# A channel shuffle on one core: two early tiles stored in pieces, large tiles moved as even and odd partitions

## The chip, the core and the metric

The kernel runs on one core of a Trainium2 chip. The metric is the device time of one execution in microseconds (us); lower is better. KB in this text is 1024 bytes and, where a tile or a piece is named by its size, it is the size per partition: a "38 KB tile" has 38 KB in each of the 128 partitions, 4864 KB in all.

## The reference

```python
def reference(x, groups):                 # x: (16, 64, 64, 256) float32, groups = 8
    batch, h, w, c = x.shape
    channels_per_group = c // groups      # 32
    x = x.reshape(batch, h, w, groups, channels_per_group)
    x = x.transpose(0, 1, 2, 4, 3)
    return x.reshape(batch, h, w, c)
```

Each of the 65,536 pixels has 256 channels (1 KB). They are taken as an 8 by 32 matrix and transposed to 32 by 8. Nothing is added or multiplied: 67.11 MB are read from HBM, permuted inside every 1 KB row, and 67.11 MB are written back.

## The kernel before, in words

The pixels lie one after another in HBM and are cut into slots, `_SLOTS = [[4, 8], [28]] + [[38]] * 12 + [[16]]`. A slot's number is how many pixels each of the 128 partitions holds, so that a 38 slot is one tile of 38 KB in each partition, and partition p's 38 KB are contiguous in HBM. The numbers add up to 512 pixels per partition, which is the whole input. The first slot has two parts of 4 and 8 KB in one tile.

For every slot there is an `in_tile` from a pool of two buffers (`_IN_BUFS`) and an `out_tile` from a pool of three (`_OUT_BUFS`). Each part goes through three steps:

- L55, issued by SyncE (SP): one DMA loads the part from HBM into `in_tile`.
- L57, VectorE (DVE): one copy from `in_tile` to `out_tile` does the permutation, by its access patterns.
- L61, issued by ScalarE (ACT): one DMA stores the part from `out_tile` to HBM.

Nothing is put in order by hand beyond that (`tc.manual_schedule(engines=None)`): every engine takes its own instructions in the order in which the loop issues them, and the framework adds the waits. It finds them from the parts of tiles that instructions read and write. A load into a buffer waits for the copy that read it two slots earlier. A copy waits for its load, and for the store that read its `out_tile` buffer three slots earlier. A store waits for its copy. A DMA reports that it has landed on one of eight semaphores (`DMAHW0` to `DMAHW7`), which are used again and again; a DMA that takes one over waits until the DMA that had it last has landed.

SP and ACT have a DMA queue each (q1 carries the loads, q10 the stores), and both queues are served by the same 16 DMA engines. A DMA of 128 partitions is cut into 128 packets, one for each partition, 8 on each engine, and ends with a 4-byte packet on each engine that counts the semaphore up.

Of the kernel before, what the change touches and what calls it, by code (L numbers as in the profile page):

```python
# [1 line left out]

# [4 lines left out]


F32 = mybir.dt.float32
P = 128  # L10

_SLOTS = [[4, 8], [28]] + [[38]] * 12 + [[16]]
_IN_BUFS = 2
_OUT_BUFS = 3


@with_exitstack
def kernel(
    ctx: ExitStack,
    tc: tile.TileContext,  # L20
    x: bass.AP,
    groups: bass.AP,
    out: bass.AP,
):
    nc = tc.nc
    b, h, w, c = x.shape
    G = int(groups)
    CPG = c // G
    assert G * CPG == c
    assert sum(map(sum, _SLOTS)) * P == b * h * w  # L30
    biggest = max(map(sum, _SLOTS))

    x_flat = x.rearrange("b h w c -> (b h w c)")
    out_flat = out.rearrange("b h w c -> (b h w c)")

    in_pool = ctx.enter_context(tc.tile_pool(name="in_pool", bufs=_IN_BUFS))
    out_pool = ctx.enter_context(tc.tile_pool(name="out_pool", bufs=_OUT_BUFS))

    def rows(flat, first, q):

        return flat[first * c : (first + P * q) * c].rearrange("(p f) -> p f", p=P)

    ctx.enter_context(tc.manual_schedule(engines=None))
    first = 0
    for parts in _SLOTS:
        in_tile = in_pool.tile([P, biggest * c], F32, name="in_tile")
        out_tile = out_pool.tile([P, biggest * c], F32, name="out_tile")
        at = 0
        pieces = []
        for q in parts:  # L50
            pieces.append((q, first, slice(at * c, (at + q) * c)))
            first += P * q
            at += q
        for q, start, cols in pieces:
            nc.sync.dma_start(out=in_tile[:, cols], in_=rows(x_flat, start, q))  # L55
        for q, start, cols in pieces:
            nc.vector.tensor_copy(  # L57
                out=out_tile[:, cols].rearrange("p (i j g) -> p i j g", j=CPG, g=G),
                in_=in_tile[:, cols].rearrange("p (i g j) -> p i j g", g=G, j=CPG),
            )  # L60
            nc.scalar.dma_start(  # L61
                out=rows(out_flat, start, q), in_=out_tile[:, cols]
            )


# [1 line left out]
_INS = ['x', 'groups']  # L67
_OUTS = [((16, 64, 64, 256), 'float32')]

_NUMBERS = {'groups': 8}  # L70


# [26 lines left out]
```

## Time and profile before

| what | value |
|---|---|
| median of 3 runs | 316.21 us (316.19 to 316.47) |
| span of the profiled execution, first to last instruction | 314.4 us |
| last DMA packet ends, last completion arrives (from the span's start) | 313.3 us, 313.6 us |
| VectorE busy | 119.0 us, 38%, 16 copies |
| DMA engines busy, loads and stores | 49.8% and 49.4% of the span |
| moved | 134.22 MB, mean 427 GB/s |

The span is the profiled execution's own time between its first and last instruction. The page has no second clock around it; the median of the runs lies 1.8 us above the span, and that difference is taken as what lies around the span in every execution. VectorE is idle most of the time, and all of that idle time ends with a load that lands. Times below are counted from the span's start.

### The profile page before, as it was taken

Reading aid. Unit: us, or ns where it says so; the run is one execution under the profiler, and the core shown is the slowest. Engines: PE = TensorE matmul, PEld = TensorE weight load, DVE = VectorE, ACT = ScalarE, POOL = GpSimd, SP = SyncE. Lnnn points to the kernel's source line nnn. Section 1 sums busy time; section 2 is a strip of 40 time slices with the busy share of each in tenths; the row PEclk is TensorE's granted clock in tenths of the full one; section 3 lists DMA queues with packets and bytes.
Section 4 is the critical chain, followed back from the end, with each engine's and each line's share of the span. In section 5 each row is a group of like instructions: output and inputs, shape, how many; then the busy total and the mean of one; then the engine's idle time right before and its main releaser. Section 6 shows DMA issues by size and latency. Waiting matters only on the chain.

```text
span 314.4 us, 132 instructions
## 1 busy us (share of the span) xinstructions
DVE 119.0 (38%) x16; POOL 0.2 (0%) x4
## 2 busy tenths in 40 slices
DVE  2081907309109109019028028037046055065400
POOL 0000000000000000000000000000000000000000
DMA  7999999999999999999999999999999999999997
GB/s 317 405 441 416 435 416 483 401 465 406 450 421 446 426 436 436 401 470 396 475 396 475 396 470 401 470 401 470 401 450 421 446 426 436 436 417 450 429 421 321
DMA packets 4608, 134.22 MB, mean 427 GB/s; under 512 B 512, under 2 KB 512, under 8 KB 768
## 3 DMA queue, kind: packets, MB, share of 16 engines
q1 hardware_dynamic: 2304, 67.11, 49.8%
q10 hardware_dynamic: 2304, 67.11, 49.4%
HBM read 67.11 MB, written 67.11 MB: 427 GB/s over the span
## 4 chain that ended last, share of the span: by engine, by line
DMA 76%; DVE 19%; issue 0%; SPq 0%; DVEq 0%
DMA in_tile<-in_x_dram 76%; DVE out_tile L57 19%; SPq L55 0%; DVEq L57 0%
## 5 line engine op out<-in xcount | busy, mean ns | idle before, releaser
L57 DVE COPY out_tile<-in_tile 128x9728 f32<-128x9728 f32 (+4 forms) x16 | 119.0, 7440 | 179.4 <-DMA in_tile<-in_x_dram 179.4
L80 POOL MEMSET const-uint8-127<- 128x1 uint8 x1 | 0.1, 103 | 0.0
L80 POOL MEMSET const-bfloat16-1.0<- 128x1 bf16 x1 | 0.1, 102 | 0.0
L80 POOL MEMSET const-float32-1.0<- 128x1 f32 x1 | 0.1, 100 | 0.0
L80 POOL MEMSET const-float32-0.0<- 128x1 f32 x1 | 0.1, 99 | 0.2 <-issue 0.2
## 6 DMA issues: line engine op xcount, KB each, us to landing
in_tile<-in_x_dram SPq DMA_DIRECT2D x12, 4864.0 KB, 37.0
out_dram<-out_tile ACTq DMA_DIRECT2D x12, 4864.0 KB, 42.6
in_tile<-in_x_dram SPq DMA_DIRECT2D x1, 3584.0 KB, 14.7
out_dram<-out_tile ACTq DMA_DIRECT2D x1, 3584.0 KB, 30.9
in_tile<-in_x_dram SPq DMA_DIRECT2D x1, 2048.0 KB, 30.4
out_dram<-out_tile ACTq DMA_DIRECT2D x1, 2048.0 KB, 15.2
in_tile<-in_x_dram SPq DMA_DIRECT2D x1, 1024.0 KB, 5.4
out_dram<-out_tile ACTq DMA_DIRECT2D x1, 1024.0 KB, 25.0
```

The costliest lines, as they stand in the source:

```text
L57: nc.vector.tensor_copy(out=out_tile[:, cols].rearrange("p (i j g) -> p i j g", j=CPG, g=G), in_=in_tile[:, cols].rearrange("p (i g j) -> ...
L80: nc = _bacc.Bacc("TRN2", target_bir_lowering=False, num_devices=1)
```

## The change

Two things change, on the way into and out of SBUF.

A dictionary `_CUTS = {2: [12, 16], 3: [16, 22]}` names the third part (the 28 KB tile) and the fourth (the first 38 KB tile). Each of them is still loaded as a whole, and is then copied and stored in two pieces: copy of 12 KB, its store, copy of 16 KB, its store; and 16 and 22 KB for the first 38 KB tile.

Every 38 KB tile is loaded by two DMAs, one for the 64 even partitions and one for the 64 odd ones, and is stored by two, the odd ones first. The copies still cover all 128 partitions. Loads have 28 DMAs where they had 16, stores 31 where they had 16, and there are 18 copies where there were 16.

```diff
+_CUTS = {2: [12, 16], 3: [16, 22]}
...
+    def classes(q):
+
+        if q < biggest:
+            return [slice(0, P)]
+        return [slice(0, P, 2), slice(1, P, 2)]
...
+    done = []
     for parts in _SLOTS:
...
         for q, start, cols in pieces:
-            nc.sync.dma_start(out=in_tile[:, cols], in_=rows(x_flat, start, q))
+            source = rows(x_flat, start, q)
+            for rank in classes(q):
+                nc.sync.dma_start(out=in_tile[rank, cols], in_=source[rank, :])
         for q, start, cols in pieces:
-            nc.vector.tensor_copy(
-                out=out_tile[:, cols].rearrange("p (i j g) -> p i j g", j=CPG, g=G),
-                in_=in_tile[:, cols].rearrange("p (i g j) -> p i j g", g=G, j=CPG),
-            )
-            nc.scalar.dma_start(
-                out=rows(out_flat, start, q), in_=out_tile[:, cols]
-            )
+            target = rows(out_flat, start, q)
+            lo = 0
+            for width in _CUTS.get(len(done), [q]):
+                part = slice(cols.start + lo * c, cols.start + (lo + width) * c)
+                nc.vector.tensor_copy(
+                    out=out_tile[:, part].rearrange(
+                        "p (i j g) -> p i j g", j=CPG, g=G
+                    ),
+                    in_=in_tile[:, part].rearrange(
+                        "p (i g j) -> p i j g", g=G, j=CPG
+                    ),
+                )
+                for rank in reversed(classes(q)):
+                    nc.scalar.dma_start(
+                        out=target[rank, lo * c : (lo + width) * c],
+                        in_=out_tile[rank, part],
+                    )
+                lo += width
+            assert lo == q
+            done.append(q)
```

In the changed kernel the loads are at L65, the copies at L71 and the stores at L80.

## The prediction

> **What bounds the kernel now.** I read the page first, then the chain of work that ended last, the copies by shape, and the packet records of the trace. On the page the two queue rows matter most.
>
> ```profile
> span 314.4 us, 132 instructions
> ...
> DVE 119.0 (38%) x16; POOL 0.2 (0%) x4
> ...
> DMA  7999999999999999999999999999999999999997
> GB/s 317 405 441 416 435 416 483 401 465 406 450 421 446 426 436 436 401 470 396 475 396 475 396 470 401 470 401 470 401 450 421 446 426 436 436 417 450 429 421 321
> ...
> q1 hardware_dynamic: 2304, 67.11, 49.8%
> q10 hardware_dynamic: 2304, 67.11, 49.4%
> ```
>
> The packets take 49.8% + 49.4% = 99.2% of 16 engines' span, 311.9 us of 314.4. The DMA engines never starve except in the first and the last of the 40 slices. What is idle, 2.5 us, is mostly the way to the first packet (1.75 us in the packet records) and the end. The engines are the bound; VectorE is busy 38% and costs nothing as long as the queues hold work. Same bytes, same packets: the loads cost 0.4 points (1.26 us) more than the stores. The packet records place this in the first 21 us, where loads run with few stores beside them; after that a 38 KB packet takes 1.44 us either way.
>
> From the stores' row an engine set that is never idle moves 67.11 MB in 0.494 x 314.4 = 155.3 us, 432 GB/s: 1 KB in each of 128 partitions is 0.303 us, a 38 KB tile 11.5 us.
>
> The chain shows what the queues hold when a copy runs:
>
> ```profile
> 8.66 21.50 DMA in_tile<-in_x_dram
> 30.16 0.02 issue
> 30.18 8.83 DVE out_tile L57
> 39.02 0.02 issue
> 39.03 32.20 DMA in_tile<-in_x_dram
> ```
>
> The first 38 KB tile is copied from 30.18 to 39.0, and only then is the third 38 KB load issued. That costs nothing, because the second 38 KB load is in flight (its copy starts at 49.11 in the timeline) and the stores of the 8 and 28 KB parts are queued. This cover is what I ask after for the changed kernel.
>
> ```profile
> L57 DVE COPY out_tile<-in_tile 128x9728 f32<-128x9728 f32 x12 | 105.5, 8791 | 158.5 <-DMA in_tile<-in_x_dram 158.5
> L57 DVE COPY out_tile<-in_tile 128x7168 f32<-128x7168 f32 x1 | 6.6, 6569 | 7.7 <-DMA in_tile<-in_x_dram 7.7
> L57 DVE COPY out_tile<-in_tile 128x4096 f32<-128x4096 f32 x1 | 3.9, 3873 | 7.6 <-DMA in_tile<-in_x_dram 7.6
> ```
>
> These rows (busy us, mean ns of one) price the pieces: 16 KB (4096 elements) 3.87 us; 22 KB (5632) between the rows of 4096 and 7168, 3.87 + 1536 x 0.878 ns = 5.22 us.
>
> **The change, part by part.** *More DMAs and packets.* 59 DMAs instead of 32: 27 more, each with one 4-byte completion packet per engine, 9 ns in the packet records: 0.24 us. The cut tiles have 16 more data packets per engine: two packets of 12 and 16 KB (459 ns by line between 309 and 611, and 611) against one of 28 KB (1062) cost 8 ns more, 16 + 22 against 38 KB about 10 ns: 8 x 18 ns = 0.14 us. Sum 0.38 us, all of it on the bound. Below nothing is excluded, since packets are only added.
>
> *More issues.* One DMA instruction takes 0.33 us on SP and 0.36 us on ACT (the rows of L55 and L61): 12 more on SP, 15 more on ACT. Behind an extra load on SP stands the next load, which waits for a copy anyway, and four packets of 1.44 us per engine of the first half are queued by then; behind an extra store, the next store, some 20 us away. Nothing, and without this cover 0.33 to 0.36 us each.
>
> [...] 32 DMAs back to back leave 0.8% of the span idle, so a completion is not paid at the queue while another DMA is queued. [...]
>
> *The pieces of the 28 KB tile.* Copy of 12 KB, then 16 KB without a wait; the stores go behind that of 8 KB. Order changes, not bytes: 0.
>
> *The pieces of the first 38 KB tile.* Here the instructions of the built program have something that the diff does not show. Rows 3 to 7 of VectorE and 5 and 6 of ACT, with what each waits for:
>
> ```
> 3 L71 TensorCopy out_tile<-in_tile 128x3072 [waits DMAHW3_49]
> 4 L71 TensorCopy out_tile<-in_tile 128x4096
> 5 L71 TensorCopy out_tile<-in_tile 128x4096 [waits DMAHW5_49,DMAHW0_49]
> 6 L71 TensorCopy out_tile<-in_tile 128x5632 [waits DMAHW3_49,DMAHW2_49]
> ...
> 5 L80 DMACopy out_dram<-out_tile 64x4096 [waits DMAHW2_49,DVE_49]
> 6 L80 DMACopy out_dram<-out_tile 64x4096 [waits DMAHW3_49]
> ```
>
> The 22 KB copy (row 6) waits for DMAHW3 and DMAHW2 at 32, their second completion: the even and the odd half of the 16 KB piece's store. It writes other columns than the store reads, so the data don't ask for it; the 28 KB tile's second copy, beside a store of whole partitions, has no such wait. So the 22 KB copy starts when the 16 KB store has *landed*. Behind it on VectorE stands every later copy, and so the second tile's store; SP's third 38 KB load waits for this copy (it frees the in_tile buffer), ACT's next store is its own. All that can still move before it: loads of 4, 8, 28, 38, 38 KB and stores of 4, 8, 12, 16, 16 KB. That is 172 KB x 0.303 = 52.1 us. With the first packet at 1.75 and the 1.26 us that early loads cost, the engines run dry at 55.1. VectorE is long ready: the 16 KB copy ends at 30.2 + 3.9 = 34.1, and its store is last in the queue. The second load's odd half takes over the semaphore of the 8 KB store, which landed at 8.66 + 25.0 = 33.6 before; four packets of its even half are queued beyond that: 0.
>
> Then nothing moves: last packet to completion 0.34 (313.28 to 313.62 in the packet records at the end), semaphores on VectorE 0.09 (0.04 + 0.05 in the chain's rows), the copy 5.22, 0.02, and from the next issue to its first packet 1.02 (issue at 0.73, packet at 1.75). Sum 6.69 us with all 16 engines idle. By the bounds of landing (0.02 as in the chain's "issue" rows; 0.9 if engines end as far apart as the last 1.1 us of the span allow) 6.4 to 7.3. No cover gives it back: the engines are the bound to the end. After it, load 3 (11.5 us) and the 22 KB store (6.7) make 18.2 us of work, while the copy of load 2, 8.8 us, ends and issues more.
>
> *Waits in the steady part.* A store now takes over the semaphore of the store two tiles back. Tiles come every 23.0 us (copies at 94.33 and 117.35), stores land 42.6 us after issue, so 46 - 42.6 = 3.4 us remain; if they are used up, the previous store is still queued: 0.
>
> *Half the partitions.* No row shows a DMA of 64 partitions. A 38 KB packet stays a contiguous 38 KB row, and 64 rows make four per engine if all 16 take part. Nearest row: 1.439 us for 1536 store packets, almost without spread. I take that: 0. A gain is excluded, as packets already run at the engine's constant time; for a loss the next rows are the slowed early loads, 1.09 against 1.06 us, 3%.
>
> Sum against the profiled execution: 314.4 + 0.38 + 6.69 = 321.5 us of span; with 1.8 us around it, against the median, 316.21 + 7.07 = 323.3 us.
>
> **The rivals.** *Halves run slower* (0.12). The halves carry 12 tiles x 2 x 11.5 = 276 us of engine time, so 1% is 2.8 us and 3% 8.3 us: 326 to 332, more if engines get in each other's way. For it: nothing measured speaks on 64 partitions. Against it: packets keep size and number. [...]
>
> *The pieces pay* (0.03, the other side). If stores that start earlier mix in while loads run alone, the 1.26 us vanish: 316.21 - 1.26 + 0.38 = 315.3. It decides only if the 22 KB copy's wait is free, that is if 6.7 us of other work were queued at 55 us; what I count there is none. *The wait is satisfied early and nothing else moves* (0.03): 316.6, within 0.2%. For these speaks that the wait stands in no line of the diff; against both, the built rows.
>
> **How the numbers follow.** The drained queue has 0.82; its own range is 322.6 to 324.2. The predicted time is its 323.3. The range adds 0.8 below for a store order that leaves work over, and reaches into the slower halves up to 328; beyond it I leave 0.06 below and some 0.07 above. About 0.2% (0.6 us) is what a measurement can tell from no change: faster 0.03, same 0.03, slower 0.94.
>
> **What would show it.** Right: the DMA row, all nines now, has a hole of 6 to 7 us between about 55 and 62 us, in slices 6 and 7; a 22 KB copy of 5.2 us whose wait, put down to DMA out_dram<-out_tile, is some 21 us; the queue shares sum to about 312.3 us; 38 KB packets stay at 1.44 us. Wrong: no hole (the wait is free), a second hole later (a semaphore taken over late), or queue shares above 313 us (halves run slower).

## The result and the profile after

The changed kernel takes 327.31 us (median of 4 runs, 327.15 to 327.43) against 316.20 us: slower, ratio 1.0348, 95% interval 1.0334 to 1.0363. It is 11.1 us longer. (In this text medians are over all runs of a kernel, and ratios with their intervals over its fast runs alone, those within 1.5% of its fastest.) The prediction, 323.3 us, had the direction and the place, and 7.1 of the 11.1 us.

The page of the changed kernel, the lines that answer to those of before:

```profile
span 325.5 us, 176 instructions
...
DVE 120.1 (37%) x18; POOL 0.2 (0%) x4
...
DMA  8989997399999999999999999999999999999995
GB/s 334 443 370 456 427 417 324 115 416 405 461 411 435 411 445 435 407 450 445 402 454 435 407 459 435 407 459 435 407 459 435 407 454 435 411 457 404 464 408 256
...
q1 hardware_dynamic: 2496, 67.11, 48.8%
q10 hardware_dynamic: 2800, 67.11, 47.8%
```

A slice is 8.1 us, and slices are counted from 0. The DMA row, before all nines but for its two ends, falls to 7 and 3 in slices 6 and 7, from 48.8 to 65.1 us, and ends with a 5 where it ended with a 7. The queues' packets took 96.6% of 325.5 us, 314.4 us, where they took 311.9.

The chain of waits of the changed kernel between 34 and 63 us (start, length, what) shows the hole from inside:

```profile
34.52 0.52 ACTq L80
35.04 0.04 issue
35.08 20.85 DMA out_dram<-out_tile
...
56.02 5.26 DVE out_tile L71
61.29 0.02 issue
61.30 0.47 SPq L65
61.78 0.04 issue
61.82 20.33 DMA in_tile<-in_x_dram
```

The 16 KB piece's store (two DMAs, one for each half) is issued from 34.52 on and has landed at 55.93; only then does the 22 KB copy run; only after that copy is the next load issued. The list of waits names it too: VectorE waited for a store once, for 21.5 us.

```profile
DVE out_tile L71 <- DMA in_tile<-in_x_dram: 167.6, 15, 15.0
DVE out_tile L71 <- DMA out_dram<-out_tile: 21.5, 1, 21.5
```

The stretches around it (length, busy time of VectorE and GpSimd, clock, DMA share, GB/s):

```profile
48.00:56.00 8.00, 0.00 (x0) 0.00 (x0) 1.00 0.88 377
56.00:64.00 8.00, 7.98 (x2) 0.00 (x0) 1.00 0.29 78
64.00:72.00 8.00, 5.93 (x1) 0.00 (x0) 1.00 0.91 369
```

From 56 to 64 us VectorE is busy all the time and the DMA engines for 29% of it: for this once the engines wait for VectorE, for the 5.25 us of its 22 KB copy.

I split the 11.1 us by the packet records of the two profiles, as time of all 16 engines (sums over packets divided by 16). The records name no engine: what is said of single engines here and below is read from the order in which packets start and from the last 16 completion packets.

| term | before | after | more |
|---|---|---|---|
| engines idle near 55 us | 0 | 7.4 us | 7.4 |
| load packets beyond the usual time of their size (38 KB: 1.439 us) | 1.1 | 3.2 | 2.0 |
| engines idle at the end, behind the last one | 0.3 | 1.6 | 1.3 |
| more packets and completions | | | 0.4 |

The second and third terms were not in the prediction. Of the 2.0 us, 1.3 lie between 60 and 80 us: the first 16 load packets after the hole take 1.7 to 2.8 us each instead of 1.44. At the end twelve engines are done by 322.4 us and four at 323.3 to 324.2; before, all 16 ended between 312.85 and 313.28.

### The profile page after: what moved, and what is told of

Same layout as the page of the kernel before. It is cut to its first block, busy times and chain, and to the rows that moved or that the text cites. A ratio compares the mean times of both kernels' runs of the same rounds, so it can differ in the third digit from the quotient of the medians.

```text
span 325.5 us, 176 instructions
## 1 busy us (share of the span) xinstructions
DVE 120.1 (37%) x18; POOL 0.2 (0%) x4
## 3 DMA queue, kind: packets, MB, share of 16 engines
q1 hardware_dynamic: 2496, 67.11, 48.8%
## 4 chain that ended last, share of the span: by engine, by line
DMA 75%; DVE 18%; SPq 1%; issue 0%; ACTq 0%; DVEq 0%
DMA in_tile<-in_x_dram 69%; DVE out_tile L71 18%; DMA out_dram<-out_tile 6%; SPq L65 1%; ACTq L80 0%; DVEq L71 0%
## 5 line engine op out<-in xcount | busy, mean ns | idle before, releaser
L71 DVE COPY out_tile<-in_tile 128x9728 f32<-128x9728 f32 (+5 forms) x18 | 120.1, 6682 | 189.2 <-DMA in_tile<-in_x_dram 167.6
```

Source lines behind the costliest of these rows:

```text
L71: nc.vector.tensor_copy(out=out_tile[:, part].rearrange("p (i j g) -> p i j g", j=CPG, g=G), in_=in_tile[:, part].rearrange("p (i g j) -> ...
```

## The experiments

Two theories on what lies beside the hole. Theory A: it belongs to the restart, and more widely to any stretch in which the load queue runs dry and all engines take up loads again. Theory B: it belongs to the half-partition DMAs. Each kernel was timed beside the kernel before on the same chip.

**The halves alone.** `_CUTS = {}`.

> The changed kernel without the two cuts: every 38 KB tile still moves as even and odd partitions, swapped for stores. In the changed kernel the copy's wait left the DMA engines idle for 7.4 us; 4 us more are lost elsewhere: 38 KB load packets after that hole take up to 2.8 us instead of 1.44 (2.0 us of 16 engines in sum) and the last engine ends 1.3 us later behind the others than before. Theory A (restart): both come from the restart after the hole, when all 16 engines begin loads together. Then halves alone cost only their 24 extra completions, 0.22 us: 316.4 us, no hole, 38 KB loads at a mean of 1.445 us as before. Theory B (halves): engines that carry half the partitions get in each other's way whenever loads run in step. Then 317.5 to 319.5 us, no hole, 38 KB load packets over 1.5 us in some number, engines ending over 1 us apart.

Measured: 316.17 us, ratio 0.9997 (0.9988 to 1.0005). The queue rows of its page:

```profile
span 314.4 us, 168 instructions
...
DMA  8999999999999999999999999999999999999997
...
q1 hardware_dynamic: 2496, 67.11, 49.8%
q10 hardware_dynamic: 2496, 67.11, 49.5%
```

24 more DMAs raise the stores' share by 0.1 point and nothing else. The 38 KB loads have a mean of 1.443 us, and all engines end within 0.5 us. Theory B falls for even and odd halves as this change moves them.

**The pieces alone.** `classes()` returns the whole 128 partitions always; both cuts stay.

> Only the cuts: the 28 KB and the first 38 KB tile copied and stored in pieces, every DMA over all 128 partitions. No copy of a second piece waits for the first piece's store in the built program. Both theories: no hole; 16 more data packets per engine (0.14 us) and 2 more DMAs (0.02 us) against at most 1.2 us of slowed early loads that earlier stores could relieve: 316.3, between 315.4 and 316.5 us.

Measured: 318.25 us (single runs 317.1 to 321.9), ratio 1.0065 (1.004 to 1.009). A miss for both theories as I had put them: no hole, no halves, and still 2.1 us. The list of waits of this kernel:

```profile
DVE out_tile L69 <- DMA in_tile<-in_x_dram: 130.5, 12, 16.6
DVE out_tile L69 <- DMA out_dram<-out_tile: 37.1, 3, 22.9
```

Copies wait for stores here, up to 22.9 us: an `out_tile` is not free. The reason lies in turns. Where both queues hold work, the records show an engine taking a load packet, a store packet, a load packet, whatever their sizes, with now and then two of a kind in a row: in the kernel before, five times from 34.6 to 47.1 us, 16 store packets of 28 KB start and then 16 load packets of 38 KB; in the changed kernel, from 32.96 to 36.9 us, 16 of 12 KB and then 16 of 38 KB, twice. Whole, the 28 KB tile's store has 8 packets per engine; in two pieces it has 16, and each lets a 38 KB load pass. Its chain of waits:

```profile
23.08 42.34 DMA out_dram<-out_tile
65.43 0.03 issue
65.45 0.05 DVEq L69
65.50 0.04 issue
65.55 8.84 DVE out_tile L69
```

The 16 KB rest of the 28 KB tile, issued at 23.1, lands at 65.4; the whole tile before landed 30.9 us after its issue at 22.9, at 53.8. The second 38 KB cut adds to it, and the copy that needs the `out_tile` of the first 38 KB tile starts at 97.26. The loads meanwhile have run ahead into both `in_tile` buffers: in the records no 38 KB load packet is active from 95.0 to 110.9 us. The stores go on: the copies at 97.26 and 108.68 us had both waited for one to land. But after it load packets beyond 1.5 us appear again (0.5 us in sum), some stores too (0.3 us), and one engine ends 1.2 us behind the other fifteen.

**The change without the false wait.** The stores of the first 38 KB tile's pieces go over 128 partitions.

```diff
-                for rank in reversed(classes(q)):
+                for rank in reversed(classes(width)):
```

> The whole change except that the two pieces of the first 38 KB tile are stored over all 128 partitions, so that the 22 KB copy no longer waits for the 16 KB store; everything else moves as even and odd partitions. My account of the hole: the 7.4 us go, and nothing else is late in their place. Theory A (restart): the rest goes with it, 316.6 us. Theory B (halves): some of the 4 us stay, 317.5 to 320 us. If the hole had another cause, it stays near 327.

Measured: 318.05 us, ratio 1.0055 (1.0043 to 1.0067). The hole is gone and 9.3 of the 11.1 us with it, which shows that the wait was its cause. The loads run dry twice here, from 53 to 61 and from 80 to 85 us, while the stores go on, and two engines end 1.6 to 1.8 us behind the rest. What holds these loads back is a store too: SyncE waited for one three times, up to 21.9 us, before it issued a load. The first 16 load packets after the two stretches took 1.44 to 1.46 us, not the 1.7 to 2.8 us that they took after the hole.

**The hole alone.** All loads whole, and only the stores of the first 38 KB tile's pieces in halves.

```diff
-            for rank in classes(q):
+            for rank in [slice(0, P)]:
...
-                for rank in reversed(classes(q)):
+                for rank in reversed(classes(q if len(done) == 3 else 0)):
```

> The hole alone: both cuts, only the first 38 KB tile's two pieces stored as odd and even partitions (so the 22 KB copy waits for the 16 KB store), all loads and all other stores over 128 partitions. Both theories: a hole of 7 to 7.5 us near 55 us. Theory A (restart): loads after the hole are slowed and engines end apart as in the changed kernel, 326 to 327 us. Theory B (halves): loads after the hole run at 1.44 us, 323.5 to 324.3 us.

Measured: 326.02 us, ratio 1.0298 (1.0282 to 1.0314). The hole is there (7.2 us), and so is what follows it, with loads of 128 partitions: 1.3 us of slowed loads between 60 and 80 us, the first packets 1.6 to 2.9 us, and one engine 1.7 us late. From the pieces alone (318.25 us) this kernel differs only in how the two pieces of the first 38 KB tile are stored, and it takes 7.8 us more. That is theory A's number, as far as it speaks of the restart after the hole.

**A late load in the kernel before.** No pieces, no halves; the load of slot 8 waits one copy longer.

```diff
+        if slot in _LATE:          # {7}
+            nc.vector.tensor_copy(out=scratch[:, :], in_=held[:, 0:8])
+        held = in_tile
```

> The kernel before, with no pieces and no halves, and one load held back: a copy of 8 elements per partition reads the in_tile of slot 6 once more after slot 7's copy, so that the load of slot 8 starts one copy later (its result is used for nothing). The load queue then runs dry for about 11 us near 140 us while the stores go on, so the DMA engines never stop. Theory A, as the pieces alone now suggest it (318.25 us with no hole, loads dry from 94 to 110 us): a stretch in which only stores run, after which all engines take up loads again, slows some 38 KB loads beyond 1.5 us and leaves one or two engines 1 to 2 us behind until the end: 317.2 to 318.5 us. Rival C: the pieces cost by themselves (short packets, more DMAs), and a dry load queue costs nothing: 316.2 us, all 38 KB loads after 30 us at 1.44 us.

Measured: 320.66 us (three runs at 320.4 to 320.7, one at 331.6), ratio 1.0133 (1.0115 to 1.0151), with no hole. Rival C falls: a dry load queue does cost. But my picture of the cost was a miss: the engines end together, and it is the *stores* that are slowed, lastingly. The stretch from 200 to 280 us, here and then in the kernel before:

```profile
200.00:280.00 80.00, 26.45 (x3) 0.00 (x0) 1.00 1.01 417
```

```profile
200.00:280.00 80.00, 28.16 (x4) 0.00 (x0) 1.00 1.00 432
```

The engines are as busy and move less: store packets there take 1.58 us instead of 1.44, 3.7 us in sum. The records of starts, ranked within each tile, show what changed. Before, an engine's load stands two packets further in its tile than its store; from about 190 us on, when the store queue takes up work again after it stood empty from 177.1 to 189.9 us, both stand at the same place in their tiles, and only from then on are stores slow. The wider half of theory A fails here: the first 16 loads after the dry stretch (138.3 to 153.7 us) took 1.44 to 1.47 us. The slow first loads (up to 2.8 us in the changed kernel, 2.9 with the hole alone) belong to a restart in which all engines stood idle, and not to every dry load queue.

**One cut at a time**, over 128 partitions: `{2: [12, 16]}` and `{3: [16, 22]}`.

> Only the 28 KB tile is cut (12 and 16 KB), all DMAs over 128 partitions. Stores and loads take turns packet by packet, so a tile in two pieces costs the stores 8 more turns; one cut alone should not put them far enough behind for a copy to wait for its out_tile with the load queue empty. Theory A: loads never run dry, 316.1 to 316.4 us. Rival C: half of what both cuts cost, about 317.2 us.

> Only the first 38 KB tile is cut (16 and 22 KB), all DMAs over 128 partitions, so that the second copy has no wait for the first store. Theory A: loads never run dry, 316.1 to 316.4 us. Rival C: about 317.2 us.

Measured: 316.11 us (0.9993, 0.9985 to 1.0002) and 316.13 us (0.9996, 0.9987 to 1.0004). Neither costs or gains; in neither is a load packet slowed beyond 60 us. The 2.1 us of both need both, as the turns have it.

**Lower and upper halves.** No cuts; `slice(0, P // 2)` and `slice(P // 2, P)`.

> No cuts; every 38 KB tile travels as partitions 0 to 63 and 64 to 127 (stores the upper ones first) where the change takes even and odd ones. Even and odd halves alone measured 316.17 us, as before. If a DMA of 64 partitions costs nothing whichever they are: 316.2 us, 38 KB packets at 1.44 us. [...]

Measured: 456.61 us, ratio 1.4313 (1.4246 to 1.4379). The profiled execution was the longest of six (449.2 to 459.9 us):

```profile
span 458.1 us, 168 instructions
...
q1 hardware_dynamic: 2496, 67.11, 56.2%
q10 hardware_dynamic: 2496, 67.11, 42.0%
```

56.2% of 458.1 is 257 us for the loads, where the kernel before took 157, and 42.0% is 192 us for the stores, where it took 155. The engines are full (98.2% of the span) and slow: 38 KB loads at a median of 2.51 us, where the kernel before has 1.44. So a DMA of 64 partitions does not cost nothing whichever they are: the even and odd halves measured 0.9997, these 1.4313. What in the lower and the upper halves slows the packets the runs don't show.

**The whole change with one of the two cuts.**

> The whole change except that the 28 KB tile is not cut. The 22 KB copy still waits for both halves of the 16 KB piece's store. My account of the hole: the same 172 KB per partition are all that can move before it, so the hole of 7.2 to 7.5 us stays, near 55 us, and what follows it too: 325 to 327.5 us. If the hole needed the cut of the 28 KB tile: 316 to 318 us.

> The whole change except that the first 38 KB tile is not cut: no copy waits for a piece's store. No hole. A queue replayed by turns, with this kernel's waits, has the loads run dry for some 5 us near 55 us, because two halves of a load take over semaphores of stores that are late. Theory A (a dry load queue costs afterwards): 316.8 to 318.5 us. If only the pieces' number or the halves counted, which cost nothing one by one: 316.2 us.

Measured: 326.90 us (1.0341, 1.0327 to 1.0354) with the 38 KB cut, and 317.90 us (1.0055, 1.0042 to 1.0068) with the 28 KB cut. The first has the hole (7.3 us) and almost all of the loss: halves and the 38 KB cut make it together, neither alone. In the instructions built with lower and upper halves instead (not timed), or with whole stores, the 22 KB copy has no wait for the store: it comes from the step over every second partition. The second has no hole, but its loads run dry from 53 to 62 us, while the stores go on, and again two engines end 1.3 to 1.5 us behind the others. SyncE issued the even half of the third 38 KB load at 39.58 and the odd half only at 56.84: in the built instructions that half takes over the semaphore of the store of the 28 KB tile's 16 KB piece, which landed at 56.8. So the 28 KB cut, free over 128 partitions, costs 1.8 us beside halves.

**Halves in the same order.** Even first for loads and stores: `reversed` is taken out, no cuts.

> No cuts, even and odd partitions for loads and stores alike in the same order (even first), where the change stores the odd ones first. If the swap of the order matters, this differs from the 316.17 us of the halves alone; nothing in the traces says that it does: 316.1 to 316.3 us.

Measured: 328.09 us, ratio 1.0381 (1.0366 to 1.0396); expected 316.2. A miss by 12 us: the swap that I had passed over carries the halves.

```profile
span 325.9 us, 168 instructions
...
q10 hardware_dynamic: 2496, 67.11, 51.2%
q1 hardware_dynamic: 2496, 67.11, 48.1%
```

The stores take 51.2% of 325.9 us, 166.9 us against 155.3, which is the whole loss; their 38 KB packets have a mean of 1.556 us. The ranks show load and store of an engine at the same place in their tiles, as with the late load, and the excess per store packet is the same: 0.14 to 0.15 us from 60 us on here, 0.14 us there. With the swap (halves alone) the places coincide too, but one side is at even and the other at odd partitions, and the excess is 0.

**A later late load.** `_LATE = {10}`.

> As the late load of before (320.66 us), but the load of slot 11 is held back instead of that of slot 8, so that the loads run dry for 11 us near 210 us instead of 140. There, nothing was slowed until 185 us, and from then to 280 us the stores beside loads lost 0.9 to 1.0 us in each 20 us, 3.9 us in sum. If a dry load queue leaves a lasting change behind, the cost shrinks with the time that is left, some 25 of 95 us: 316.5 to 317.5 us. If it is one price for each restart: 319.5 to 321 us. If the late load had cost for another reason (its extra copy): 320.5 us too, but with no slowed packets after 230 us.

Measured: 317.24 us, ratio 1.0051 (1.0029 to 1.0074). The cost shrinks with the time that is left, as it should if the late load leaves a change behind, and not a fixed price of 4.5 us. That the change is the same one is not shown: runs lay between 317.0 and 322.5 us, and the profiled one was the longest. In it stores beside loads are slow too (1.50 to 1.52 us on average from 250 us on), but with loads and stores at places one or two packets apart, so the same place may not be the whole condition.

## Why the prediction was right, and where it fell short

**The bound and the wait: right.** Only time taken from the DMA engines counted, and the wait that stood in the built instructions and not in the diff took it. Predicted were a dry queue at 55.1 us, a copy wait of 21 us and a copy of 5.22; measured 55.3, 21.5 and 5.25. Taking the wait away (318.05) and putting it in without halved loads (326.02, against 318.25 without the wait) both confirm it.

**The hole's size: 6.69 predicted, 7.4 measured.** The copy was right. From the engines' last packets (55.33 us on average) to the landing it was 0.6, not 0.34, and from the next issue (61.30) to the engines' first packets (62.8 on average) 1.5, not 1.02.

**What was missing: the restart, 3.3 us.** "No cover gives it back", I wrote, and stopped there. I counted when the engines start again, not how. In all three kernels with a hole the first 16 loads, which begin within 0.4 to 1.4 us of each other with no stores between them, took 1.6 to 2.9 us, and the last engine ended 2.1 to 2.3 us behind the first. The slowest engine ends the run: in the changed kernel the last packet ends at 324.2 us, of a span of 325.5. Why an engine that falls behind there does not catch up, no run here tests.

**"Order changes, not bytes: 0" for the pieces: true for each cut over 128 partitions, wrong for both.** Twice the packets take twice the turns: with both cuts the last of the 28 KB tile landed at 65.4 us instead of 53.8. It doesn't show in the sum: in the changed kernel every store that is queued has landed when the hole begins.

**Semaphores taken over late: 0, true with the hole only.** I asked whether the second load and the steady stores have to wait for one. With the hole gone (318.05), and with the 28 KB cut beside halves (317.90), a load does, for up to 21.9 and for 16.8 us, and the load queue runs dry.

**The halves: 0, right, for a reason I hadn't given.** I took 0 because packets stay 38 KB; that holds for lower and upper halves too, which cost 133 to 144 us, and for even and odd ones in the same order, which cost 12. The rival *halves run slower* was refuted for this change by the halves alone, though its sign came: I had named queue shares above 313 us as its mark, they were 314.4, and they came from the restart. The measured time lies in the part of the range that this rival had opened, so that the range held was luck. *The pieces pay* fell with 316.11 and 316.13: earlier stores didn't give back the slow early loads.

**More packets and completions: 0.38, right.** 0.14 and 0.24 us in the records.

**The slow early loads: one reading was off.** I placed their 1.26 us in the first 21 us. The packet records give 1.14 us beyond the usual time of each size, 0.66 of it before 21 us and 0.47 between 21 and 49 us. The sum doesn't change by it, since all of it lies before the queue ran dry.

**What stays open.** Which resource slows a load at a restart from idle, why one or a few engines fall behind there and also after a dry load queue with no slow first loads, and whether a store beside a load at the same place is slowed in SBUF or in HBM. The runs show when it happens. No kernel here beats the one before beyond what a run can tell (best 316.11, interval up to 1.0002).

## What to carry to other kernels

Before changing how a DMA walks a tile, read the waits of the built instructions: here a store over every second partition was taken to touch columns that a copy wrote, and the copy waited for it. Where the DMA engines are full all the time, count what is queued at each new wait, and add the restart to the idle time (here 3.3 us beside 7.4). Count turns, not only bytes: here, with both cuts alone, the 28 KB tile's store in 16 packets per engine instead of 8 landed at 65.4 us instead of 53.8, and the loads of 38 KB packets ran ahead into both `in_tile` buffers (none active from 95.0 to 110.9 us).

## What the runs showed of the hardware that I had not expected

- Even and odd partitions cost nothing (0.9997), lower and upper halves 1.43 times the time, at the same packet sizes.
- A store packet of 38 KB takes 1.58 us instead of 1.44 while, by the order of starts, its engine's loads stand at the same place in their tile (late load, halves in the same order); at other places, or on partitions of the other parity, 1.44 us in every trace but that of the later late load. In the halves this is 12 us of 316, decided by the order of two DMAs.
- After a stretch in which all engines stood idle the first 16 load packets of 38 KB took 1.6 to 2.9 us (three kernels), and the engines, which had ended within 0.5 us of each other, ended up to 2.3 us apart. After a stretch without loads in which the stores went on, the first 16 took 1.44 to 1.47 us in three kernels and up to 1.95 us in a fourth (the pieces alone).
